# Mixer: the conformer branch goes last of the four, and its convolution taps are written one a step

## The chip, the cores and the metric

The kernel runs on one core of one Trainium2 chip. The metric is the device time of one execution in microseconds (us). The core has five engines that each take their own queue in order: TensorE (PE in the rows; PEld are its weight loads), VectorE (DVE), ScalarE (ACT), GpSimd (POOL) and SyncE (SP), which issues the loads of weights.

## The reference

A model of four layers on 256 tokens of width 1024. The first two layers are blocks of a feed-forward part, a mixer, and a feed-forward part; the last two are attention layers. The change lies in the mixer, which stands once in each of the first two layers:

```python
u = rms_norm(h, mix_pre_g[l])
(a_b, a_c, a_x, b_u, c_q, c_k, c_v,
 d_q, d_k, d_v, d_f, gate_logits) = _split(u @ w_in[l], IN_SPLITS)
y_a = short_conv_mixer(...)          # 3 taps
y_b = conformer_conv_mixer(...)      # 31 taps, then layer_norm, silu, output product
y_c = diff_attention_mixer(...)
y_d = forgetting_attention_mixer(...)
g = sigmoid(gate_logits)             # 4 x 1024 columns
merged = g[:, :, 0] * y_a + g[:, :, 1] * y_b + g[:, :, 2] * y_c + g[:, :, 3] * y_d
h = h + rms_norm(merged @ w_o[l], mix_post_g[l])
```

Branch b, the conformer branch:

```python
y = a * sigmoid(g)
y = causal_depthwise_conv(y, conv_w) + conv_b     # 31 taps over 512 channels
y = silu(layer_norm(y, ln_g, ln_b))
return y @ w_out
```

## The kernel before

**Products.** All large products run in a split form. `Stream` loads the weights in pieces of 128 x 1024 numbers in the order in which they are planned (four raw buffers, loads issued by SyncE), ScalarE rounds each piece to its high part `whi` (L95), VectorE subtracts to get the low part `wlo` (L96), and there are eight such pairs of buffers. A block of 128 tokens by 512 columns then takes three matmuls for each chunk of 128 rows: high by high, low by high, high by low (L396, L397, L399). A panel is 512 columns for both halves of the tokens (t = 0 and 1), that is two blocks; a block has eight chunks, or four for a branch's output product. The results stand in two PSUM banks of the pool `mm`; four other banks (`acc`) hold logits and attention outputs, two (`tr`) transposes.

**Steps.** Inside a block, `slot()` is called after every two chunks and at the end: that is one step. A step splits weights ahead, runs deferred work, and then has a purse: `RATE` = 0.8 is added, up to 1.6, and small pieces of work are taken from the list `work` (attention of c and d, the normalisation of b), and then from `filler`, as long as the purse is above 0. Each piece names its price in its `yield`. The convolution of b is the only filler: `conv_b` issues, for each of four channel blocks, one multiply (L615) and 30 taps (L617) on VectorE, with a `yield` behind each tap. When all are written, it starts `norm_b` for both halves of the tokens: transposes of the convolved tile `cb` (L624), statistics (L626, L628), a power on GpSimd (L263), normalised tile `lnx` (L631), transposes of it (L278), scale and shift (L637), tanh (L639, ScalarE), product (L643), and the high and low parts of `bt` (L292 on ScalarE, L293 on VectorE), which the output product of b reads.

**Order.** The mixer first computes its input panels, then for each branch in `BRANCHES`: a gate panel, an output panel, a second gate panel, a second output panel. After a branch's first gate panel, `finish(b)` writes all that is left of its work at once. The first branch writes the merged tile, the next two multiply by their gate on VectorE (L861) and add on GpSimd (L862), the last adds on VectorE and defers the transposes for the final product. The program as written gives each instruction its rank; the compiler that builds the engines' queues takes them by rank, but draws a later one forward where it finds the engine free and the instruction ready. What stands in a queue then runs in that order.

Of the kernel before, what the change touches and what calls it, by code (L numbers as in the profile page):

```python
# [29 lines left out]
RATE = 0.8  # L30
WINDOW = 8

BRANCHES = ["a", "d", "b", "c"]
GATE_OFF = {"a": 5640, "b": 5640 + DM, "c": 5640 + 2 * DM, "d": 5640 + 3 * DM}
FF_PANELS = [(i * 512, 512) for i in range(DFF // 512)]
FF_LAST = (DFF // 512 * 512, DFF % 512)
# [89 lines left out]
def encoder_kernel(ctx, tc, I, C, out, upto=None):  # L126
# [46 lines left out]
    def cols(w, c0, n):  # L173
        return (w[:, c0 : c0 + n], n)
# [9 lines left out]
    for l in range(DEPTH):  # L184
        plan_ffn(l, 1)
        for nm, (c0, n) in MIX_PANELS.items():
            W.plan((l, "m", nm), [cols(I["w_in"][l], c0, n)], KD)
        for b in BRANCHES:
            for i in range(2):
# [17 lines left out]
    def defer(fn, d=4):  # L207
        later.append((clock[0] + d, fn))
# [10 lines left out]
    def start(name, gens):  # L219
        work.extend([0, name, g] for g in gens)  # L220
# [15 lines left out]
    def finish(name):  # L236
        for q in (filler, work):
            while True:
                mine = [w for w in q if w[1] == name][:WINDOW]
                if not mine:  # L240
                    break
                for w in mine:
                    step(q, w)
# [58 lines left out]
    def to_T(src, X, t, c0=0, n=4, scale=None):  # L302

        p = tr_ps()
        tr(p, src, n)
        split_ps(c3(p, n), X[0][:, c0 : c0 + n, tb(t)], X[1][:, c0 : c0 + n, tb(t)], scale)
        X[2].update((c, t) for c in range(c0, c0 + n))
# [186 lines left out]
    def mixer(l, U, rs, tab, nxt):  # L494
# [116 lines left out]
        def conv_b():  # L611
            assert filled.count(30) == NTB
            cb = x4_p.tile([P, 4, SEQ], F32, tag="x4", name="cb")
            for c in range(4):
                V.tensor_scalar(out=cb[:, c], in0=yb[:, c, 0:SEQ], scalar1=cw[:, c, 0:1], scalar2=cw[:, c, 31:32], op0=ALU.mult, op1=ALU.add)  # L615
                for j in range(1, 31):
                    V.scalar_tensor_tensor(out=cb[:, c], in0=yb[:, c, j : j + SEQ], scalar=cw[:, c, j : j + 1], in1=cb[:, c], op0=ALU.mult, op1=ALU.add)  # L617
                    yield 0.33, 0
            start("b", [norm_b(cb, t) for t in range(NTB)])

        def norm_b(cb, t):
            p = tr_ps()
            for c in range(4):
                T.transpose(p[:, c * P : (c + 1) * P], cb[:, c, tb(t)], ident)  # L624
            bs = small("bst", 6)
            V.bn_stats(out=bs, in_=p)  # L626
            mv = small("bmv", 2)
            V.bn_aggr(out=mv, in_=bs)  # L628
            r = rpow(mv[:, 1:2], tag="ln")
            x = t2("lnx")  # L630
            V.tensor_scalar(out=x, in0=p, scalar1=mv[:, 0:1], scalar2=r, op0=ALU.subtract, op1=ALU.mult)  # L631
            yield 1.4, 4
            q = tr_ps()
            tr(q, x)
            v = t2("lnv")
            for c in range(4):
                V.tensor_scalar(out=v[:, tb(c)], in0=q[:, tb(c)], scalar1=cw[:, c, 32:33], scalar2=cw[:, c, 33:34], op0=ALU.mult, op1=ALU.add)  # L637
            th = t2("lnt")
            S.activation(th, v, AF.Tanh, scale=0.5)  # L639
            if "b" not in OT:  # L640
                OT["b"] = pair4("bt")
            yield 0.8, 1
            V.scalar_tensor_tensor(out=v, in0=th, scalar=1.0, in1=v, op0=ALU.add, op1=ALU.mult)  # L643
            split_ps(c3(v, 4), OT["b"][0][:, :, tb(t)], OT["b"][1][:, :, tb(t)], 0.5)
            OT["b"][2].update((c, t) for c in range(4))
            yield 1.2, 1
# [58 lines left out]

        panel(key("dv"), U, 520, ev_dv)
        filler.append([0, "b", conv_b()])
        panel(key("dq"), U, 512, ev_T(dqk[:, 0], "dq"))
        panel(key("dk"), U, 512, ev_T(dqk[:, 1], "dk"))
# [136 lines left out]
        MT = None  # L846
        for b in BRANCHES:
            for i in range(2):
# [7 lines left out]
                def ev_out(t, p):  # L856
                    m = M[:, t, sl]
                    if b == BRANCHES[0]:
                        V.scalar_tensor_tensor(out=m, in0=gt[t], scalar=1.0, in1=p, op0=ALU.add, op1=ALU.mult)
                    else:  # L860
                        V.scalar_tensor_tensor(out=gt[t], in0=gt[t], scalar=1.0, in1=p, op0=ALU.add, op1=ALU.mult)  # L861
                        (V if b == BRANCHES[-1] else G).tensor_tensor(out=m, in0=m, in1=gt[t], op=ALU.add)  # L862
                    if b == BRANCHES[-1]:
                        defer(lambda m=m, i=i: to_T(m, MT, t, c0=4 * i, scale=0.5), 3)

                panel(key("g" + b, i), U, 512, ev_gate)
                if i == 0:
                    finish(b)
                if b == BRANCHES[0] and i == 0:
                    M = b8_p.tile([P, NTB, DM], F32, tag="b8", name="merged")  # L870
# [440 lines left out]
```

## Time and profile before

| | |
|---|---|
| time, 3 runs | 1676.97 us median (1676.76 to 1680.42) |
| the profiled execution | 1680.77 us, of it span 1679.0 us |
| busy: TensorE, VectorE, ScalarE, GpSimd | 97%, 66%, 52%, 6% of the span |
| mean granted TensorE clock | 0.995 of full speed |

A busy share is an average over the span. What a wait costs is read on the engine that has no slack, TensorE here; the rows below show its waits in the mixer and the work of other engines beside them.

### The profile page before, as it was taken

How to read it: one execution, taken by the hardware profiler on the slowest of the kernel's cores; microseconds unless marked ns; L12 is line 12 of the kernel's file. 1: busy time of each engine (PE TensorE's matmuls, PEld its weight loads, DVE VectorE, ACT ScalarE, POOL GpSimd, SP SyncE). 2: the span in 40 equal slices, each digit the busy share in tenths (PEclk: the TensorE clock that was granted, in tenths of full speed). 3: DMA queues.
4: the chain of work that ended last, by engine and by line, in shares of the span. 5: the costliest groups of instructions: out<-in, count | busy, mean ns of one | idle time of the engine just before them, and what ended most of it. 6: DMA issues, size and time to landing. Idle time of an engine off the chain costs nothing. (4 is left out here: it accounts for less than half of the span.)

```text
span 1679.0 us, 21707 instructions
## 1 busy us (share of the span) xinstructions
PE 1631.7 (97%) x7949; PEld 1344.5 (80%) x7949; DVE 1114.2 (66%) x1802; ACT 871.9 (52%) x1349; POOL 108.9 (6%) x114
## 2 busy tenths in 40 slices
PE   7999999899999999999999998999999998999998
PEld 6888888778887888888887877788888887788686
DVE  6555566997666555565546599975665556887885
ACT  6544456564545454454535466644455445644653
POOL 0000000101100000000000010011010002100100
PEclk9999999999999999999999999999999999999999
DMA  7756556445665655566565573556475554533520
GB/s 272 228 183 204 170 178 202 130 119 183 190 200 173 213 180 197 152 225 198 174 205 182 150 226 101 168 193 191 153 233 174 188 196 133 177 97 114 151 76 26
DMA packets 141602, 289.83 MB, mean 173 GB/s; under 512 B 12374, under 2 KB 26478, under 8 KB 141240
## 3 DMA queue, kind: packets, MB, share of 16 engines
q1 hardware_dynamic: 140856, 285.82, 53.6%
q0 software_dynamic: 352, 2.11, 0.3%
q8 instruction: 62, 1.02, 0.2%
q10 hardware_dynamic: 288, 0.52, 0.1%
q14 instruction: 44, 0.36, 0.1%
HBM read 287.35 MB, written 1.06 MB: 172 GB/s over the span
## 5 line engine op out<-in xcount | busy, mean ns | idle before, releaser
L96 DVE TENSOR_TENSOR wlo<-raw,whi 128x1024 fp32r<-128x1024 f32 (+2 forms) x532 | 639.8, 1209 | 314.0 <-ACT whi L95 297.4
L95 ACT CAST whi<-raw 128x1024 fp32r<-128x1024 f32 (+2 forms) x532 | 547.8, 1036 | 407.5 <-PE mm L399 212.2
L396 PE MATMUL mm<-whi,uh 128*128 128x512 f32 (+2 forms) x1504 | 594.7, 396 | 1.8 <-ACT sq L1010 1.3
L399 PE MATMUL mm<-whi,ul 128*128 128x512 f32 (+2 forms) x1504 | 580.5, 386 | 0.4 <-DVE ul L293 0.4
L397 PE MATMUL mm<-wlo,uh 128*128 128x512 f32 (+2 forms) x1504 | 580.1, 386 | 0.0
L399 PEld LDWEIGHTS mm<-whi,ul 128*128 128x128 f32 x1504 | 283.5, 188 | 58.1 <-DVE ul L293 0.9
L396 PEld LDWEIGHTS mm<-whi,uh 128*128 128x128 f32 x1504 | 283.7, 189 | 57.8 <-issue 4.5
L397 PEld LDWEIGHTS mm<-wlo,uh 128*128 128x128 f32 x1504 | 284.1, 189 | 51.1 <-issue 1.0
L396 PE MATMUL acc<-whi,hth 128*128 128x512 f32 x352 | 137.4, 390 | 0.0
L397 PE MATMUL acc<-wlo,hth 128*128 128x512 f32 x352 | 137.0, 389 | 0.0
L617 DVE SCALAR_TENSOR_TENSOR cb<-yb,cw,cb 128x256 f32<-128x256 f32 x240 | 109.7, 505 | 0.5
L399 PE MATMUL acc<-whi,htl 128*128 128x512 f32 x352 | 108.8, 390 | 0.0
L397 PEld LDWEIGHTS acc<-wlo,hth 128*128 128x128 f32 x352 | 66.1, 188 | 13.7
L396 PEld LDWEIGHTS acc<-whi,hth 128*128 128x128 f32 x352 | 66.1, 188 | 13.7
L399 PEld LDWEIGHTS acc<-whi,htl 128*128 128x128 f32 x352 | 65.8, 188 | 13.5
L289 ACT CAST hth<-tr 128x512 fp32r<-128x512 f32 (+1 forms) x48 | 26.3, 548 | 63.4 <-PE tr L278 63.4
L475 DVE SCALAR_TENSOR_TENSOR hx<-mm,rs,sg 128x512 f32<-128x512 f32 x40 | 29.9, 746 | 43.3 <-PE mm L399 43.3
L263 POOL TENSOR_TENSOR post<-postm,nhalf 128x1 f32<-128x1 f32 x12 | 8.7, 724 | 743.9 <-DVE postm L259 743.9
L290 DVE TENSOR_TENSOR htl<-tr,hth 128x512 fp32r<-128x512 f32 (+1 forms) x48 | 30.8, 643 | 38.2 <-ACT hth L289 38.2
L854 ACT ACTIVATE gate<-mm,hrs 128x512 f32<-128x512 f32 x32 | 22.0, 687 | 47.5 <-PE mm L399 47.5
L270 ACT ACTIVATE junk<-acc 128x512 bf16<-128x512 f32 x24 | 14.1, 593 | 50.3 <-PE acc L399 50.3
L471 ACT ACTIVATE sg<-mm,rs 128x512 f32<-128x512 f32 x40 | 27.6, 690 | 17.7 <-PE mm L399 17.5
(356 smaller groups left out, 1674.7 us busy)
## 6 DMA issues: line engine op xcount, KB each, us to landing
raw<-in_w_in_dram SPq DMA_DIRECT2D x180, 512.0 KB
raw<-in_ffn_w_down_dram SPq DMA_DIRECT2D x88, 512.0 KB
raw<-in_ffn_w_gate_dram SPq DMA_DIRECT2D x80, 512.0 KB
raw<-in_ffn_w_up_dram SPq DMA_DIRECT2D x80, 512.0 KB
raw<-in_w_o_dram SPq DMA_DIRECT2D x16, 512.0 KB
raw<-in_w_out_dram SPq DMA_DIRECT2D x16, 512.0 KB
raw<-in_w_in_dram SPq DMA_DIRECT2D x16, 260.0 KB
raw<-in_ffn_w_gate_dram SPq DMA_DIRECT2D x16, 256.0 KB
```

Source lines behind the costliest of these rows:

```text
L95: self.nc.scalar.copy(hi[:, : ks * n], src)
L96: self.nc.vector.tensor_tensor(out=lo[:, : ks * n], in0=src, in1=hi[:, : ks * n].bitcast(F32), op=ALU.subtract)
L270: S.activation(j[:, :w], src, AF.Square, scale=scale, accum_out=acc)
L289: S.copy(hi, p)
L290: V.tensor_tensor(out=lo, in0=p, in1=hi.bitcast(F32), op=ALU.subtract)
L396: T.matmul(o, lhsT=X[0][:, xk, tb(t)], rhs=a, start=first, stop=False)
L397: T.matmul(o, lhsT=X[0][:, xk, tb(t)], rhs=b, start=False, stop=False)
L399: T.matmul(o, lhsT=X[1][:, xk, tb(t)], rhs=a, start=False, stop=last)
L471: S.activation(sg[t], p, AF.Silu, scale=rs[t])
L475: V.scalar_tensor_tensor(out=x, in0=p, scalar=rs[t], in1=sg[t], op0=ALU.mult, op1=ALU.mult)
L617: V.scalar_tensor_tensor(out=cb[:, c], in0=yb[:, c, j : j + SEQ], scalar=cw[:, c, j : j + 1], in1=cb[:, c], op0=ALU.mult, op1=ALU.add)
L854: S.activation(gt[t], p, AF.Tanh, scale=hrs[t])
```

## The change

Two lines. In `BRANCHES` the branches b and c change places, so that gate and output panels of b come last; the weights are planned by the same list. In `conv_b` the price of a tap goes from 0.33 to 0.75, so that with 0.8 a step about one tap is written in a step instead of two or three.

```diff
-BRANCHES = ["a", "d", "b", "c"]
+BRANCHES = ["a", "d", "c", "b"]
...
                 for j in range(1, 31):
                     V.scalar_tensor_tensor(out=cb[:, c], in0=yb[:, c, j : j + SEQ], scalar=cw[:, c, j : j + 1], in1=cb[:, c], op0=ALU.mult, op1=ALU.add)
-                    yield 0.33, 0
+                    yield 0.75, 0
```

On VectorE, at the first softmax of branch d (first mixer), where taps stand among weight splits (`wlo`) and the softmax instructions (L721, two rows for each of four heads), there stands before:

```order
L617 SCALAR_TENSOR_TENSOR cb<-yb,cw,cb 128x256 x3
L96 TENSOR_TENSOR wlo<-raw,whi 128x1024
L617 SCALAR_TENSOR_TENSOR cb<-yb,cw,cb 128x256 x13
L721 ISA de,dnm<-L,T_2153 128x256
L721 ISA dnm 128x1
L721 ISA de,dnm<-L,T_2153 128x256
L721 ISA dnm 128x1
L721 ISA de,dnm<-L,T_2153 128x256
L721 ISA dnm 128x1
L721 ISA de,dnm<-L,T_2153 128x256
L721 ISA dnm 128x1
L617 SCALAR_TENSOR_TENSOR cb<-yb,cw,cb 128x256
```

and now, from the same softmax to the next one:

```order
L617 SCALAR_TENSOR_TENSOR cb<-yb,cw,cb 128x256 x11
L721 ISA de,dnm<-L,T_2153 128x256
L721 ISA dnm 128x1
L721 ISA de,dnm<-L,T_2153 128x256
L721 ISA dnm 128x1
L721 ISA de,dnm<-L,T_2153 128x256
L721 ISA dnm 128x1
L721 ISA de,dnm<-L,T_2153 128x256
L721 ISA dnm 128x1
L617 SCALAR_TENSOR_TENSOR cb<-yb,cw,cb 128x256 x4
L615 TENSOR_SCALAR cb<-yb,cw 128x256
L617 SCALAR_TENSOR_TENSOR cb<-yb,cw,cb 128x256
```

Two taps fewer stand in the run ahead of the first softmax (39 in all since the first tap, 41 before), three more behind it (before: one tap, the multiply, one tap), and a weight split follows there that stood behind the second softmax before.

On TensorE, at the same place, transposes of the exponentials (`de`) and logits (`L`) stand among the matmuls of a panel (`mm`); before:

```order
L278 MATMUL tr<-ident,qk 128x128 x4
L748 MATMUL tr<-ident,de 128x128 x4
L717 MATMUL L<-dqk 128x128 x4
L396 MATMUL mm<-whi,uh 128x512
L397 MATMUL mm<-wlo,uh 128x512
L399 MATMUL mm<-whi,ul 128x512
L396 MATMUL mm<-whi,uh 128x512
L397 MATMUL mm<-wlo,uh 128x512
L399 MATMUL mm<-whi,ul 128x512
L748 MATMUL tr<-ident,de 128x128 x8
L717 MATMUL L<-dqk 128x128 x4
```

and now:

```order
L278 MATMUL tr<-ident,qk 128x128 x4
L396 MATMUL mm<-whi,uh 128x512
L397 MATMUL mm<-wlo,uh 128x512
L399 MATMUL mm<-whi,ul 128x512
L396 MATMUL mm<-whi,uh 128x512
L397 MATMUL mm<-wlo,uh 128x512
L399 MATMUL mm<-whi,ul 128x512
L748 MATMUL tr<-ident,de 128x128 x4
L717 MATMUL L<-dqk 128x128 x8
```

Six matmuls moved ahead of the first transposes of `de`, and the last four logits moved ahead of the next transposes of `de`. Between the first and the second set of logits twelve matmuls stand now, six before; behind the second set the numbers are the other way round, six ahead of the transposes of `qk` and twelve before.

On TensorE, at the normalisation of branch b, before (the matmuls are those of branch d's first output panel):

```order
L396 MATMUL mm<-whi,dt 128x512
L397 MATMUL mm<-wlo,dt 128x512
L399 MATMUL mm<-whi,dt 128x512
L624 MATMUL tr<-ident,cb 128x128 x8
L396 MATMUL mm<-whi,dt 128x512
L397 MATMUL mm<-wlo,dt 128x512
L399 MATMUL mm<-whi,dt 128x512
```

and now (the matmuls ahead are the last of b's first gate panel, those behind the first of b's output panel):

```order
L396 MATMUL mm<-whi,uh 128x512
L397 MATMUL mm<-wlo,uh 128x512
L399 MATMUL mm<-whi,ul 128x512
L624 MATMUL tr<-ident,cb 128x128 x8
L278 MATMUL tr<-ident,lnx 128x128 x8
L396 MATMUL mm<-whi,bt 128x512
L397 MATMUL mm<-wlo,bt 128x512
L399 MATMUL mm<-whi,bt 128x512
```

Before, 24 matmuls stand between the two sets of transposes and 114 between the second set and the first matmul that reads `bt`; now there is none in either place.

On VectorE, in the same normalisation, before:

```order
L96 TENSOR_TENSOR wlo<-raw,whi 128x1024 x5
L626 BN_STATS bst<-tr 128x6 x2
L628 BN_AGGR bmv<-bst 128x2
L861 SCALAR_TENSOR_TENSOR gate<-gate,mm 128x512
L261 TENSOR_SCALAR lnm<-bmv 128x1
L628 BN_AGGR bmv<-bst 128x2
L261 TENSOR_SCALAR lnm<-bmv 128x1
L631 TENSOR_SCALAR lnx<-tr,bmv,ln 128x512 x2
L861 SCALAR_TENSOR_TENSOR gate<-gate,mm 128x512
L96 TENSOR_TENSOR wlo<-raw,whi 128x1024 x2
L637 TENSOR_SCALAR lnv<-tr,cw 128x128 x8
```

and now:

```order
L96 TENSOR_TENSOR wlo<-raw,whi 128x1024 x4
L626 BN_STATS bst<-tr 128x6 x2
L628 BN_AGGR bmv<-bst 128x2
L96 TENSOR_TENSOR wlo<-raw,whi 128x1024
L261 TENSOR_SCALAR lnm<-bmv 128x1
L628 BN_AGGR bmv<-bst 128x2
L261 TENSOR_SCALAR lnm<-bmv 128x1
L631 TENSOR_SCALAR lnx<-tr,bmv,ln 128x512 x2
L637 TENSOR_SCALAR lnv<-tr,cw 128x128 x8
L643 SCALAR_TENSOR_TENSOR lnv<-lnt,lnv 128x512 x2
L293 SCALAR_TENSOR_TENSOR bt<-lnv,bt 128x4x128 x2
```

The two gating products (`gate`) are gone from the chain, one weight split stands in it instead, and the steps follow each other directly.

## Rows read from the trace of the kernel before

**Rows 1.** Page, part 1: busy us, share of span, instructions.
```profile
PE 1631.7 (97%) x7949; PEld 1344.5 (80%) x7949; DVE 1114.2 (66%) x1802; ACT 871.9 (52%) x1349; POOL 108.9 (6%) x114
```

**Rows 2.** Windows, first mixer: stretch, length, busy us by engine, PEclk, DMA.
```profile
223.00:448.00 225.00, 218.16 (x1109) 178.94 (x1108) 180.54 (x358) 130.26 (x227) 20.83 (x16) 0.98 0.53 165
```

**Rows 3.** Timeline, TensorE, d softmax: start, us, instruction, count, [idle before, releaser].
```profile
303.33 1.13 PE L717 MATMUL L<-dqk 64*128 64x256 f32 x8
...
305.99 1.14 PE L717 MATMUL L<-dqk 64*128 64x256 f32 x8
...
309.92 0.60 PE L278 MATMUL tr<-ident,qk 128*128 128x128 f32 x4
...
311.99 0.93 PE L748 MATMUL tr<-ident,de 128*128 128x128 f32 x4 [1.48 <-ACT de L722]
...
318.35 1.97 PE L748 MATMUL tr<-ident,de 128*128 128x128 f32 x8 [3.19 <-ACT cqk L313]
...
1009.63 0.93 PE L748 MATMUL tr<-ident,de 128*128 128x128 f32 x4 [1.53 <-ACT de L722]
...
1015.98 1.14 PE L748 MATMUL tr<-ident,de 128*128 128x128 f32 x8 [1.69 <-ACT cqk L313]
...
1021.08 0.66 PE L748 MATMUL tr<-ident,de 128*128 128x128 f32 x4 [1.75 <-ACT det L750]
```

**Rows 4.** Windows of low clock; the number before DMA share is PEclk.
```profile
318.00:324.80 6.80, 6.45 (x27) 5.21 (x27) 6.79 (x23) 5.82 (x16) 0.07 (x1) 0.50 0.68 192
...
1010.95:1014.30 3.35, 3.34 (x12) 2.01 (x8) 3.35 (x11) 2.91 (x10) 1.35 (x2) 0.51 0.02 5
```

**Rows 5.** Timeline, VectorE, d softmax, first layer.
```profile
305.74 5.22 DVE L617 SCALAR_TENSOR_TENSOR cb<-yb,cw,cb 128x256 f32<-128x256 f32 x13
...
310.89 0.41 DVE L721 CUSTOM_DVE_ANT_0 de<-L,T 128x256 f32<-128x256 f32 x1
...
312.66 1.37 DVE L615 TENSOR_SCALAR cb<-yb,cw 128x256 f32<-128x256 f32 x1
...
314.35 0.41 DVE L721 CUSTOM_DVE_ANT_0 de<-L,T 128x256 f32<-128x256 f32 x1
...
315.73 1.21 DVE L96 TENSOR_TENSOR wlo<-raw,whi 128x1024 fp32r<-128x1024 f32 x1
```

**Rows 6.** Timeline, GpSimd, same stretch.
```profile
312.42 1.47 POOL L741 TENSOR_TENSOR T<-T,tab 128x512 f32<-128x512 f32 x1 [11.88 <-DVE dnm L721]
```

**Rows 7.** Timeline, all engines, normalisation of branch b, first layer.
```profile
409.42 1.04 PE L624 MATMUL tr<-ident,cb 128*128 128x128 f32 x8
...
411.06 1.29 DVE L626 BATCH_NORM_STATS2 bst<-tr 128x6 f32<-128x512 f32 x2
...
412.35 0.65 DVE L861 SCALAR_TENSOR_TENSOR gate<-gate,mm 128x512 f32<-128x512 f32 x1
...
412.92 0.15 DVE L261 TENSOR_SCALAR lnm<-bmv 128x1 f32<-128x1 f32 x1
...
414.39 1.09 POOL L263 TENSOR_TENSOR ln<-lnm,nhalf 128x1 f32<-128x1 f32 x2
...
415.00 1.53 DVE L631 TENSOR_SCALAR lnx<-tr,bmv,ln 128x512 f32<-128x512 f32 x2 [1.66 <-POOL ln L263]
...
415.95 1.35 PE L278 MATMUL tr<-ident,lnx 128*128 128x128 f32 x8
...
417.06 0.47 PE L396 MATMUL mm<-whi,uh 128*128 128x512 f32 x1
...
420.42 2.63 DVE L637 TENSOR_SCALAR lnv<-tr,cw 128x128 f32<-128x128 f32 x8
...
422.97 1.47 DVE L643 SCALAR_TENSOR_TENSOR lnv<-lnt,lnv 128x512 f32<-128x512 f32 x2
...
424.19 1.14 ACT L292 ACTIVATE bt<-lnv 128x512 fp32r<-128x512 f32 x2
```

**Rows 8.** Timeline, TensorE, first matmul that reads b's result.
```profile
443.02 0.39 PE L396 MATMUL mm<-whi,bt 128*128 128x512 f32 x1
```

## The prediction

> **What bounds the kernel now.** I read the page's busy shares first: TensorE is busy 97% of the span and VectorE 66% [rows 1], so a change pays or costs only through time in which TensorE waits. Then the busy time by stretch: the mixer of the first layer, which is what the change touches, lies at about 223 to 448 us; TensorE is busy 218.16 of these 225.00 us [rows 2], so it stands idle 6.84 us, and all a better order could win back in a layer is that, and what the clock lost by it. Then the rows of TensorE with the waits ahead of them: in the first layer two waits in the softmax of branch d, 1.48 and 3.19 us, in the second layer three, 1.53, 1.69 and 1.75 us [rows 3]. Behind the waits the granted clock falls to the lower of its two levels: 0.50 for 6.80 us with 6.45 us busy in the first layer, 0.51 for 3.35 us with 3.34 us busy in the second [rows 4]. At half speed half of the busy time is lost: 3.2 and 1.7 us. The waits named and their clock are 4.67 + 4.97 + 4.9 = 14.5 us for both layers. That is the pot for a gain.
>
> The cause of these waits is VectorE: 13 taps in 5.22 us (0.40 us each) stand ahead of the first softmax instruction, which starts at 310.89 although its logits were issued at 303.33 [rows 3, 5].
>
> **The change part by part.** No instruction is added or removed; branch b's and c's weights, gate panels and output panels change places in the stream, with equal sizes, so SyncE issues the same loads of the same size in the same steps. There are two parts.
>
> *The thin spread.* A higher price per tap (0.75 for 0.33) writes the taps later in the program. But the order in which VectorE gets them hardly moves: the compiler draws ready taps forward into places where it thinks VectorE free. Ahead of the first softmax of d stand 39 taps instead of 41; the runs of 13 become runs of 14 and 11. So the softmax starts 2 x 0.40 = 0.8 us sooner, at 310.1, and its four instructions end at 311.5 (1.38 us, as from 314.35 to 315.73) [rows 5]. Behind it stand now five taps and the first multiply of a channel block (one tap, the multiply and one tap before), then a split, and then the second softmax. Six instructions at 0.40 us are 2.4 us; one of them is stretched, as the multiply is now, to 1.37 us while GpSimd's 1.47 us mask addition runs [rows 5, 6], 1.0 us more; the split is 1.21 us and the second softmax 1.38 us: its end comes at 311.5 + 3.4 + 1.2 + 1.4 = 317.5 instead of 315.7. On TensorE six more matmuls now stand ahead of the first transposes of the exponentials, so that wait (1.48 us) goes. But all eight last logits stand together behind them, and the second four need the banks that the second softmax empties. TensorE is there after two sets of logits and 24 matmuls: one set and six matmuls take 2.66 us (303.33 to 305.99), one set and twelve 3.93 us (to 309.92), so six more 1.27 us, in all 2 x 2.66 + 2 x 1.27 = 7.9 us [rows 3]; with two sets of transposes (0.60 and 0.93, the latter less the 0.2 in which the next row has begun) and four logits (0.3) that is 303.33 + 9.5 = 312.8 us. It waits 317.5 - 312.8 = 4.7 us there, against 4.67 us in two waits now. The wait changes its place and the transposes behind it may wait again, as the 1.75 us one does in the second layer; there the same working gives 4.7 us against 3.2 in the first two. Bounds: all 14.5 us gained, or 5 us more in each layer, if the new wait comes on top of the old ones rather than in their place. I take a loss of 1.0 us for both layers together, because VectorE, which is full there, has the same work before and after.
>
> *Branch b last.* Its normalisation hangs on the last tap, and the taps are over long before, around the first gate panel in both kernels. What moves is the chain from the convolved tile to the first output matmul of b. Now it runs beside matmuls of other branches: its transposes start at 409.42, and the first matmul that reads its result starts at 443.02, 17.7 us after the high part of the result is there at 425.33 [rows 7, 8]. It costs nothing. After the change it stands at the end of b's first gate panel, and on TensorE's queue nothing at all lies between: eight transposes of the convolved tile, eight of the normalised one, then the matmuls that read the result. TensorE takes its queue in order, so it waits for the whole chain. The last panel of matmuls holds both banks of the matmul pool until b's output blocks have them, so no later panel stands ahead either.
>
> The chain, from the start of the transposes, with the durations of [rows 7]: 1.64 us to the statistics (409.42 to 411.06, a weight split stands before them now too, and will). From the statistics to the first small instruction of the variance 1.86 us; in it lies a gating of 0.57 us (412.35 to 412.92), whose place a weight split of 1.21 us [rows 5] takes: 2.50 us. The power on GpSimd: 0.15 for the small instruction, 0.61 from its start to the normalising instruction (414.39 to 415.00), and 0.06 for the handover, 0.82 us. GpSimd's additions of merged tiles, in front of the power now, are gone from there: the last branch adds on VectorE. That is 4.96 us so far. 0.95 us to the transposes, half of their 1.35 us for one half of the tokens, 0.1 us handover: 6.7 us. 2.55 us from the scale and shift to the gating product (420.42 to 422.97): 9.25 us. Half of its 1.47 us, 0.08, half of the 1.14 us for the high part on ScalarE, and 0.14 to TensorE, as from the normalised tile to its transposes: 10.8 us. TensorE's own work in that time, which it has now too, is 1.04 + 1.11 us (415.95 to 417.06). So it is idle 10.8 - 2.15 = 8.65 us in a layer, 17.3 us in both. Little elsewhere can give it back: of the 6.84 us of idle time in the first mixer the two softmax waits are 4.67, so all other waits there together are 2.2 us.
>
> Bounds: without the splits in front of and inside the chain, and without the second half's scale and shift in front of the first half's product, 0.6 + 1.2 + 1.3 us less, 5.5 us a layer, 11 in all. Upwards, the transposes at half clock (1.1 more) and a split that waits for its load (some 1.5 us): 11.2 us a layer, 22.4 in all. I take 17.3, since each link has a row.
>
> *The clock.* The waits of the chain, about 4.9 and 3.5 us, are longer than those after which the clock falls now, so I expect it to fall here too. The price lies between nothing (the low stretch falls into the wait) and 3.2 us a layer, the longer stretch of [rows 4]. I take the shorter, 1.7 us: 3.3 us for both.
>
> The Trainium skill ("TensorE: Matmul & The Clock Gate", section "HAM oscillation — how this bites in real kernels") charges half of all throttled time when an engine starts cold after a wait. With the longer stretch of 6.80 us that would be 3.4 us a layer as an estimate by that page, 6.8 instead of 3.3 in the sum. The trace agrees as far as its two stretches show the lower level while TensorE is busy almost throughout; no run before the change shows a wait of 4 us in this place.
>
> **Sum.** 17.3 + 3.3 + 1.0 = 21.6 us. The profiled execution took 1680.77 us with a span of 1679.0; the runs shown have a median of 1676.97, 3.8 less. 1680.77 + 21.6 = 1702.4 for such an execution, and 1676.97 + 21.6 = 1698.6 us against the median: 1.3% slower.
>
> **Rivals.**
> 1. *The softmax waits go altogether.* For it: the first of them does lose its cause in the new order, and VectorE reaches the first softmax sooner. Against it: the eight logits now stand in front of a softmax that is later than before. Price: the pot of 14.5 us, against a chain of 17.3 us whose low clock falls into its waits: 1676.97 + 17.3 - 14.5 = 1679.8 us, no change. It decides for "not slower" from 13.9 us won back (17.3 less 0.2% of the time, 3.4 us).
> 2. *The softmax stretch gets worse.* The wait for the banks comes on top of waits of the transposes behind it, 5 us more in each layer: 1698.6 + 10 - 1 = 1707.6 us. For it: the transposes wait on copies that ScalarE does behind exponentials, as the 1.69 and 1.75 us waits do now. Against it: VectorE's work up to there is the same.
> 3. *The clock stays low longer after the chain,* as in the longer of the two stretches: 3.2 instead of 1.7 us a layer, 1701.6 us. For it: two waits within some 10 us. Against it: half of that time TensorE has nothing to lose.
>
> That the spread does not do what it says is part of the forecast, since the taps keep their places nearly.
>
> **How the numbers follow.** Forecast 0.68, rival 1 0.07, rival 2 0.13, rival 3 0.12. The range for 8 in 10 is 1688 to 1709: below, the chain at its lower bound with its clock (1676.97 + 11 less what the softmax may give), above, rival 2 with a little of rival 3. A measurement here tells about 0.2%, 3.4 us, from no change. Of rival 1 most is "no change": 0.05, and 0.02 for faster; the rest, 0.93, is slower.
>
> **What would show it.** In the profile after, each mixer should have two new waits of TensorE in a row: the transposes of the normalised tile for VectorE (about 4 to 5 us), and the first matmul that reads branch b's result for ScalarE's high part (3 to 4 us), with VectorE and GpSimd going through the chain in the durations above, and a stretch at 0.50 beside it. The 1.48 us wait ahead of the first transposes of the exponentials should be gone and one of about 5 us should stand at the last logits of d. The forecast is wrong if matmuls of a later panel run between the two sets of transposes, if the first matmul of b's result starts within 7 us of the first transposes, or if the softmax stretch of d loses its waits without new ones.

## The result, and the profile after

The changed kernel takes 1699.32 us (median of four runs, 1695.70 to 1700.53) against 1677.53 us of the kernel before on the same chip: a ratio of 1.0122, with a 95% interval of 1.0109 to 1.0135. The profiled execution took 1700.18 us with a span of 1698.4, which is 19.4 us over the span before.

The page's busy line, to be held against [rows 1]: the work on each engine is the same, and TensorE's busy time has grown by 6.3 us although it runs the same 7949 matmuls: the mean granted clock is 0.989 for 0.995.

```profile
PE 1638.0 (96%) x7949; PEld 1349.7 (79%) x7949; DVE 1110.9 (65%) x1802; ACT 872.2 (51%) x1349; POOL 112.4 (7%) x114
```

The waits of TensorE after, by what it waited for (total us, times, longest). The first and the last line lie in the softmax of d, the second and third in the normalisation of b; what is left out between lies outside the change.

```profile
PE L L717 <- DVE dnm L721: 8.6, 2, 4.3
PE tr L278 <- DVE lnx L631: 8.4, 2, 4.2
PE mm L396 <- ACT bt L292: 6.3, 2, 3.1
...
PE tr L748 <- ACT det L750: 2.9, 2, 2.1
```

The chain of b's normalisation in the first layer, all engines, from the timeline (start, us, engine, line, instruction, idle before and releaser); it answers to [rows 7, 8]:

```profile
472.61 1.03 PE L624 MATMUL tr<-ident,cb 128*128 128x128 f32 x8
...
473.68 1.29 DVE L626 BATCH_NORM_STATS2 bst<-tr 128x6 f32<-128x512 f32 x2
...
474.96 1.19 DVE L96 TENSOR_TENSOR wlo<-raw,whi 128x1024 fp32r<-128x1024 f32 x1
...
476.30 1.08 POOL L263 TENSOR_TENSOR ln<-lnm,nhalf 128x1 f32<-128x1 f32 x2 [10.54 <-DVE lnm L261]
...
476.89 1.53 DVE L631 TENSOR_SCALAR lnx<-tr,bmv,ln 128x512 f32<-128x512 f32 x2 [0.40 <-POOL ln L263]
477.85 1.94 PE L278 MATMUL tr<-ident,lnx 128*128 128x128 f32 x8 [4.21 <-DVE lnx L631]
478.98 2.64 DVE L637 TENSOR_SCALAR lnv<-tr,cw 128x128 f32<-128x128 f32 x8 [0.55 <-PE tr L278]
...
481.53 0.69 DVE L643 SCALAR_TENSOR_TENSOR lnv<-lnt,lnv 128x512 f32<-128x512 f32 x1
...
482.25 0.63 ACT L292 ACTIVATE bt<-lnv 128x512 fp32r<-128x512 f32 x1
...
482.93 0.79 PE L396 MATMUL mm<-whi,bt 128*128 128x512 f32 x1 [3.14 <-ACT bt L292]
...
1185.25 1.94 PE L278 MATMUL tr<-ident,lnx 128*128 128x128 f32 x8 [4.20 <-DVE lnx L631]
1190.33 0.79 PE L396 MATMUL mm<-whi,bt 128*128 128x512 f32 x1 [3.14 <-ACT bt L292]
```

Read it down: eight transposes, nothing on TensorE for 4.21 us, eight transposes, nothing for 3.14 us, then the matmul that took until 443.02 to come in the kernel before, with 114 matmuls of other panels ahead. VectorE goes from step to step without a pause longer than 0.55 us. The last two rows are the same two places in the second layer.

The clock falls behind these waits. Windows (stretch, length, busy time by engine, granted clock, DMA share, GB/s): the first is the chain's, the other two are in the softmax of d, as [rows 4].

```profile
477.70:487.90 10.20, 6.91 (x20) 5.42 (x21) 5.95 (x14) 2.43 (x4) 0.00 (x0) 0.51 0.12 41
317.00:320.40 3.40, 3.40 (x13) 2.79 (x13) 3.40 (x8) 3.40 (x10) 2.21 (x1) 0.51 0.75 210
1025.00:1031.80 6.80, 6.77 (x26) 5.25 (x24) 6.80 (x21) 6.11 (x19) 1.75 (x1) 0.61 0.60 183
```

The softmax of d, TensorE, after, as [rows 3]. The wait of 1.48 us ahead of the first transposes of the exponentials is gone, one of 4.32 us stands at the last logits in its place, and a wait for ScalarE's copy follows.

```profile
302.59 1.14 PE L717 MATMUL L<-dqk 64*128 64x256 f32 x8
...
316.77 1.56 PE L717 MATMUL L<-dqk 64*128 64x128 f32 x8 [4.32 <-DVE dnm L721]
...
325.19 0.66 PE L748 MATMUL tr<-ident,de 128*128 128x128 f32 x4 [2.06 <-ACT det L750]
...
407.33 0.39 PE L396 MATMUL mm<-whi,dt 128*128 128x512 f32 x1
...
1010.03 1.13 PE L717 MATMUL L<-dqk 64*128 64x256 f32 x8
...
1114.73 0.39 PE L396 MATMUL mm<-whi,dt 128*128 128x512 f32 x1
```

The first matmul that reads `dt` lies behind the same work in both kernels, so the time from the first logits to it prices the softmax stretch. The rows of before for it:

```profile
408.06 0.39 PE L396 MATMUL mm<-whi,dt 128*128 128x512 f32 x1
...
1000.93 1.13 PE L717 MATMUL L<-dqk 64*128 64x256 f32 x8
...
1104.72 0.39 PE L396 MATMUL mm<-whi,dt 128*128 128x512 f32 x1
```

First layer: 408.06 - 303.33 [rows 3] = 104.73 us before, 407.33 - 302.59 = 104.74 after. Second layer: 103.79 before, 104.70 after. The softmax stretch costs 0.0 + 0.9 us. From the first logits of layer 1 to those of layer 2 are 697.60 us before and 707.44 after, 9.84 us more, all of it behind the softmax. From there to the end of the span are 678.07 us before (1679.0 - 1000.93) and 688.37 after, 10.30 us more, 0.9 of it the softmax. So the chain with its clock costs some 9.8 and 9.4 us; the 0.7 us that the first layer started earlier goes off, and 19.4 us are left.

What the clock has of that is read from TensorE's busy time (the first number behind the length) behind the softmax, from the first matmul that reads `dt` to the next logits, in the second layer to the end of the span. Before:

```profile
408.06:1000.93 592.87, 589.41 (x2738) 486.57 (x2736) 358.94 (x427) 295.91 (x361) 31.02 (x26) 1.00 0.59 190
1104.72:1679.00 574.28, 553.15 (x2809) 458.31 (x2807) 387.60 (x690) 289.95 (x502) 52.55 (x62) 0.99 0.47 149
```

and after:

```profile
407.33:1010.03 602.70, 592.56 (x2737) 488.96 (x2736) 356.05 (x427) 296.47 (x361) 33.55 (x26) 0.99 0.58 186
1114.73:1698.40 583.67, 556.17 (x2809) 460.39 (x2807) 386.42 (x690) 290.49 (x502) 53.27 (x62) 0.99 0.47 147
```

The same matmuls (one record in 2738 apart) keep TensorE busy 3.15 and 3.02 us longer, 6.2 us in both layers. I read that as the clock's price, since the trace shows nothing else that slows them. Its idle time there grew by 6.68 and 6.37 us, a little less than the 7.35 and 7.34 us of the chain's two waits, since other waits became 0.7 and 1.0 us shorter.

### The profile page after: what moved, and what is told of

Its sections match the earlier page's. It is cut to its first block, busy times and chain, and to the rows that moved or that the text cites. A ratio compares the mean times of both kernels' runs of the same rounds, so it can differ in the third digit from the quotient of the medians.

```text
span 1698.4 us, 21691 instructions
## 1 busy us (share of the span) xinstructions
PE 1638.0 (96%) x7949; PEld 1349.7 (79%) x7949; DVE 1110.9 (65%) x1802; ACT 872.2 (51%) x1349; POOL 112.4 (7%) x114
```

## The experiments

Ratios are to the kernel before on the same chip, with 95% intervals. The changed kernel was measured once more beside the first three:

> The changed kernel once more, as a control on the chip of this call: 1697 to 1701 us by either theory.

It gave 1699.27 us against 1677.74, ratio 1.0130 (1.0116 to 1.0144).

**1. The order alone.** Branch b last, the tap at its old price.

```diff
 BRANCHES = ["a", "d", "c", "b"]
...
-                    yield 0.75, 0
+                    yield 0.33, 0
```

> Branch b last, with the old price of 0.33 a tap. Theory (the loss is the chain of b's normalisation, which stands bare on TensorE's queue at the end of b's first gate panel): it stays, and only what the spread does to the softmax of d goes, so 1697 to 1700 us, within 2 us of the changed kernel, with the two waits of about 4.2 and 3.1 us in each mixer. Rival (the thin spread costs the time, since VectorE runs taps late): 1677 to 1680 us.

Measured: 1677.71 us against 1677.74, ratio 0.9999 (0.9990 to 1.0008). My theory is wrong. The timeline shows why: with b last, the normalisation is still written beside d's output panel, and there is no wait ahead of its transposes.

```profile
407.95 1.04 PE L624 MATMUL tr<-ident,cb 128*128 128x128 f32 x8
...
414.49 1.34 PE L278 MATMUL tr<-ident,lnx 128*128 128x128 f32 x8
```

**2. The price alone.** Branch b third as before, the tap at 0.75.

```diff
 BRANCHES = ["a", "d", "b", "c"]
...
-                    yield 0.33, 0
+                    yield 0.75, 0
```

> The old order a, d, b, c with the new price of 0.75 a tap. Theory: the compiler draws taps forward anyway, and the softmax waits only change their place: 1676 to 1680 us (about +1, as the softmax stretch of the changed kernel measures). Rival (the spread costs): 1690 us or more. Second rival (the spread frees VectorE for the softmax): 1665 to 1672 us.

Measured: 1700.91 us, ratio 1.0137 (1.0120 to 1.0154): the whole loss, and the rival's case. The same two waits stand in it, behind b's gate panel, wherever that panel is:

```profile
444.64 1.94 PE L278 MATMUL tr<-ident,lnx 128*128 128x128 f32 x8 [4.20 <-DVE lnx L631]
...
449.73 0.80 PE L396 MATMUL mm<-whi,bt 128*128 128x512 f32 x1 [3.14 <-ACT bt L292]
```

**3. The changed kernel with the chain written one panel earlier.** The rest of b's work is written ahead of its first gate panel, so that the panel's 48 matmuls rank behind the chain and can be run beside it.

```diff
+                if b == BRANCHES[-1] and i == 0:
+                    finish(b)
                 panel(key("g" + b, i), U, 512, ev_gate)
```

> The changed kernel, but what is left of branch b is written ahead of its first gate panel instead of behind it, so that matmuls of that panel can run beside the normalisation. Theory: the two waits and their low clock go (about 9.8 us a layer), the small loss in the softmax stretch stays: 1677 to 1681 us. Rival (b last costs by itself, for instance by VectorE adding merged tiles or by the output panels' order): 1688 us or more.

Measured: 1679.74 us, ratio 1.0009 (1.0000 to 1.0018), as expected. The chain's waits are nearly gone, and the softmax wait of 4.3 us a layer stays, so what the softmax stretch costs is in these 2 us and nearly all of the rest was the chain:

```profile
PE L L717 <- DVE dnm L721: 8.6, 2, 4.3
...
PE tr L278 <- DVE lnx L631: 0.7, 2, 0.4
```

With these three a new theory was at hand. A step puts 0.8 into the purse; attention takes its pieces first, then the taps are written for what they cost, and only when the last tap is written is `norm_b` started. Following the program's steps from the start of the taps: at the end of d's first gate panel 72 steps are over, of the third branch's 96, of the last one's 120. The attention pieces have cost 18.04 by then. With the old price all taps (39.6) are written within the 72 steps and both normalisations in the next 24, in pieces among matmuls. At 0.75 and b third, 60.0 of 90 are spent at step 96, so 80 of 120 taps are written; with b last 79.5 at step 120, 106 taps. `finish(b)` then writes the other taps and the whole normalisation in one lump, behind b's gate panel. The compiler draws those taps forward, so that they are long done by then, but not the transposes: they stand behind the gate panel's matmuls on TensorE's queue, with nothing between them and b's output. By this theory the position of b decides only between the prices at which 96 steps don't do for the taps and 120 do (the normalisation, written in steps, takes some more): (120 x 0.8 - 18.04)/120 = 0.65 and (96 x 0.8 - 18.04)/120 = 0.49. The next two runs are at 0.55, between the two.

**4. A price of 0.55, b last, and the same with b third.**

```diff
-                    yield 0.75, 0
+                    yield 0.55, 0
```

> Branch b last, as in the changed kernel, but a tap costs 0.55. Theory of the purse: a step gives 0.8, and at the end of b's first gate panel (some 120 steps after the taps were started) 96 have been given; the taps ask 120 x 0.55 = 66 and the attention pieces some 18, 84 in all, so the normalisation is written in steps among matmuls ahead of that panel's end and no wait of 4.2 or 3.1 us stands in it: 1676 to 1681 us. Rival, a dearer tap costs by itself, whatever becomes of the normalisation (two thirds of the way from 0.33 to 0.75, a half of the loss or more): 1687 to 1698.

> The same tap price of 0.55 with branch b third, as in the kernel before. Theory of the purse: only some 96 steps lie ahead of the end of b's first gate panel, 77 have been given, the taps and attention ask 84, so the normalisation is written in one lump behind that panel, its transposes wait 4.2 us and the first matmul of b's output 3.1 us in each layer: 1696 to 1702 us. Rival, the price alone decides: the same time as the run with b last at 0.55.

Measured, on one chip: b last 1683.88 us, ratio 1.0036 (1.0024 to 1.0048); b third 1699.76 us, ratio 1.0130 (1.0117 to 1.0143). 15.9 us lie between two kernels with the same price, and the sign of the position is the opposite of what I had forecast: at this price b last is the better place, because it leaves the purse 24 more steps. The chain with b last, where the transposes of the normalised tile come in two fours among matmuls, and with b third:

```profile
460.22 0.60 PE L278 MATMUL tr<-ident,lnx 128*128 128x128 f32 x4
...
462.56 0.63 PE L278 MATMUL tr<-ident,lnx 128*128 128x128 f32 x4 [1.50 <-DVE lnx L631]
...
476.41 0.39 PE L396 MATMUL mm<-whi,bt 128*128 128x512 f32 x1
```

```profile
445.57 1.94 PE L278 MATMUL tr<-ident,lnx 128*128 128x128 f32 x8 [4.20 <-DVE lnx L631]
...
450.65 0.79 PE L396 MATMUL mm<-whi,bt 128*128 128x512 f32 x1 [3.14 <-ACT bt L292]
```

The run with b last is 3 us over what I expected and 5.9 us over the kernel before. I had not foreseen the waits of 1.50 and 1.46 us in its two chains. The softmax of d takes longer too: from the first logits to the first matmul that reads `dt` are 104.98 and 105.52 us, 2.0 us more than before in both. The waits can't simply be added, though: from the first logits of layer 1 to those of layer 2 its profiled execution is only 0.42 us longer than that of the kernel before, and 5.25 us from there to the end, so most of the loss lies in and behind the second mixer. Where the rest of it went is open.

**5. TensorE kept busy in the chain's waits.** The changed kernel with 26 more matmuls a mixer, 16 ahead of the transposes of the normalised tile and 10 behind them, whose results nobody reads. On TensorE's queue 17 came to stand ahead of these transposes, one between their two fours and eight behind.

```diff
+        def idle(n):
+            d = acc_ps("idle")
+            for _ in range(n):
+                T.matmul(d, lhsT=U[0][:, 0, 0:P], rhs=U[0][:, 0:2, :].rearrange("p k s -> p (k s)"), start=True, stop=True)
...
+            if t == NTB - 1:
+                idle(16)
             yield 1.4, 4
             q = tr_ps()
             tr(q, x)
+            if t == NTB - 1:
+                idle(10)
```

> The changed kernel with 26 matmuls more in each mixer, whose result nobody reads, put into the two waits of the normalisation (17 behind the first set of transposes, 9 around and behind the second). The chain keeps its length, TensorE's clock has no reason to fall. Theory (the low clock behind the waits costs 2.5 to 3 us a layer beside the waits): 1693 to 1696 us, and no stretch at 0.50 beside the chain. Rival (the low stretch falls into the waits and costs nothing): 1698 to 1701 us.

Measured: 1697.19 us against 1678.39, ratio 1.0107 (1.0094 to 1.0121): some 3 us less than the changed kernel's 1.0130, with intervals that overlap a little, so the gain is not clear of noise. It lies between the two expectations. The windows of the same 22 us around the chain, with the unread matmuls and in the changed kernel, show that the clock came back in part, 0.92 for 0.77:

```profile
472.00:494.00 22.00, 20.20 (x90) 15.62 (x90) 16.49 (x30) 7.28 (x10) 1.08 (x2) 0.92 0.38 120
```

```profile
472.00:494.00 22.00, 14.65 (x61) 11.67 (x60) 15.80 (x29) 7.14 (x10) 1.08 (x2) 0.77 0.34 112
```

The unread matmuls did not fill the second wait, though, and the matmuls behind it still run at the lower clock:

```profile
482.61 0.50 PE L396 MATMUL mm<-whi,bt 128*128 128x512 f32 x1 [1.44 <-ACT bt L292]
```

```profile
484.00:486.00 2.00, 2.00 (x6) 1.54 (x6) 0.13 (x1) 0.00 (x0) 0.00 (x0) 0.50 0.00 0
```

So this run does not take the low stretch away; it moves it behind the second wait and makes it shorter. Its gain of some 3 us is a part of the clock's price, not the whole, which by the busy time above is some 6.2 us. The larger part of the loss is the waiting in the chain, which stays nearly as long with the clock up: 9.87 us from the first transposes to the first matmul that reads `bt` (472.74 to 482.61), for 10.32.

**6. Three taps instead of thirty,** in the kernel before. It leaves out 27 of the 30 taps in each channel block, so its output is not the reference's; it asks what VectorE's load is worth.

```diff
-                for j in range(1, 31):
+                for j in range(1, 4):
```

> The kernel before with 3 taps instead of 30 in each channel block: 108 taps a layer left out, so the convolution isn't the reference's. Theory (the softmax waits of d and their low clock come from taps that stand ahead on VectorE): 1663 to 1668 us, the waits of 1.48, 3.19, 1.53, 1.69 and 1.75 us gone. Rival (the waits are the softmax's own chain from logits to exponentials): 1674 to 1677 us.

Measured: 1687.82 us, ratio 1.0057 (1.0044 to 1.0069): 94 us of VectorE's work less, and slower. Both expectations miss. The waits in d's softmax shrink to 1.3 us each, but the normalisation, written when the last tap is, now comes in the input panels, and its transposes wait there. The waits by what TensorE waited for, and the one in the first layer:

```profile
PE tr L278 <- DVE lnx L631: 11.4, 2, 6.2
PE tr L624 <- DVE cb L617: 6.7, 2, 3.4
```

```profile
301.06 1.11 PE L278 MATMUL tr<-ident,lnx 128*128 128x128 f32 x4 [5.25 <-DVE lnx L631]
```

It is the same lesson from the other end: the price and the number of taps set where the chain is written, and the 18.1 us that TensorE waits there outweigh what the softmax gains.

**7. Better versions?** Three tries to free d's softmax of the taps, all with b last: b's input panels and the taps behind those of c and d, with the chain written ahead of b's gate panel, at 0.75; the same at 0.45; and b's input panels between c's query and key panels, at 0.45.

```diff
-        panel(key("bg"), U, 512, ev_bg)
-        panel(key("ba"), U, 512, ev_ba)
...
-        filler.append([0, "b", conv_b()])
...
         panel(key("cv"), U, 512, ev_cv)
+        panel(key("bg"), U, 512, ev_bg)
+        panel(key("ba"), U, 512, ev_ba)
+        for _ in range(5):
+            slot()
+        filler.append([0, "b", conv_b()])
...
+                if b == BRANCHES[-1] and i == 0:
+                    finish(b)
```

> Order a, d, c, b with 0.75 a tap; b's two input panels moved behind those of c and d, so that no tap can run before the softmaxes, and b's remainder written ahead of its first gate panel. Theory: VectorE is free for the softmaxes of d and c, the taps run beside the gate and output panels of a, d and c, and the normalisation beside b's gate panel: 1663 to 1669 us, faster than both kernels. Rival (the taps then hold up splits of weights beside the gate panels): 1677 us or more.

> The run with b's input panels behind those of c and d again, b last, but a tap costs 0.45. Theory: with the dear tap two waits per layer ate the gain, 3.7 us of the transposes of the convolved tile for the last tap and 2.0 us of b's output for a gate; a cheaper tap ends the taps and the normalisation earlier among matmuls, so both go, 11 us in all, with the smaller softmax waits of that order kept: 1667 to 1672 us. Rival, the taps then stand ahead of the softmaxes again and bring the old waits back: 1676 to 1682.

> The last run with b's two input panels moved up, between c's query and key panels, and the taps started ahead of c's value panel, some 20 us earlier; b last, a tap costs 0.45. Theory: in the last run the 7.3 us of waits of output blocks for a gating product come from VectorE being full of taps (110 of 120 us between 330 and 450 us); taps that start earlier leave it some room there, and they still stand behind most of d's softmax, so these waits shrink without new ones: 1668 to 1674 us. Rival, the room on VectorE only changes its place and c's softmax now waits behind taps: 1675 to 1680 us.

Measured: 1680.24 us, ratio 1.0011 (1.0002 to 1.0021); 1675.61 us, 0.9988 (0.9979 to 0.9998); 1676.02 us, 0.9992 (0.9982 to 1.0001). None comes to what I expected: the times of the first and the third are those of their rivals, and the second lies between, just below its rival's. The waits of TensorE in the three (lines are up to three off here: L623 is the transposes of the convolved tile, L746 d's transposes of the exponentials, L864 or L862 the gating product; the L746 line is the same in all three):

```profile
PE tr L623 <- DVE cb L616: 7.4, 2, 3.7
...
PE mm L397 <- DVE gate L864: 4.1, 4, 1.8
PE tr L746 <- ACT cqk L314: 3.4, 2, 1.7
```

```profile
PE mm L397 <- DVE gate L864: 7.3, 4, 2.6
```

```profile
PE mm L397 <- DVE gate L862: 7.0, 4, 1.9
```

d's softmax waits fall to 1.7 us a layer in all three. Instead the gate panels behind the output panels of d and c wait for a gating product, which stands behind taps and weight splits on VectorE. The second is 0.1% faster than the kernel before, hardly more than can be measured; in none are TensorE's waits on VectorE gone, they only move.

## Why the prediction was right, and where it was wrong

The time and the mechanism were forecast; the part of the change that brings it was not. The signs that were named are in the profile after: waits of 4.2 us (4 to 5 were named) and 3.1 us (3 to 4) in the chain, a stretch at 0.51 beside them, and 4.3 us (about 5) at the last logits of d.

- **The failed step is the paragraph "Branch b last".** It had the chain right and what moves it wrong. It said that the chain moves behind b's first gate panel because b comes last, and that "the taps are over long before". The taps are over on VectorE, but not in the program as written, and it is there that `norm_b` is started. Experiments 1, 2 and 4 show the price to be the cause: the old price with b last costs nothing, the new price with b third costs all of it, and at 0.55 b last loses 15.9 us less than b third.
- **"The thin spread" was read on the wrong engine.** "The order in which VectorE gets them hardly moves" is right for the taps, and the price of 1.0 us for the softmax stretch met 0.9 us. But the paragraph looked at the taps' order alone and did not follow what hangs on the last of them. The order of the changed kernel, which I had, contains both edits, so it could not tell which of them moved the chain; one of the two applied alone would have. That the total came right although the wrong edit was held to bring it is owed to that order: it showed the chain's new place, whatever had put it there.
- **The chain's length was nearly met.** 10.8 us were forecast from the transposes to the first matmul, 10.32 measured (472.61 to 482.93). TensorE's own work in it was put at 2.15 us and is 2.97, mostly since the transposes of the normalised tile run at the lower clock (1.94 us for 1.35, [rows 7]), so the waits are 7.35 us a layer, not 8.65: 14.7 in both, not 17.3. The split of 1.21 us inside the chain is where it was said to be (474.96). No split waited for its load there; the 1.5 us put down for one in the upper bound are shown by no run.
- **The clock's term was too small.** 1.7 us a layer were taken, the shorter stretch of [rows 4]. The busy time of the same matmuls grew by 3.15 and 3.02 us, 6.2 in both for 3.3, and that includes the slow transposes. The low stretch is 10.20 us long, longer than the two of [rows 4], but TensorE is busy 6.91 us of it only. The section "HAM oscillation — how this bites in real kernels" of the Trainium skill's "TensorE: Matmul & The Clock Gate" counts half of the throttled time; half of the 10.20 us would be 5.1 us a layer as an estimate by it, half of the 6.91 busy us 3.5. The 3.15 and 3.02 us of the trace lie near the second: part of the stretch lies in the second wait, where a low clock costs nothing. The prediction's estimate by that page, 6.8 us in the sum, was nearer than the 3.3 us that it took.
- **The sum came out closer than its terms, and that is luck.** 14.7 + 6.2 + 0.9 us, less the 1.6 us by which other waits shrank and the 0.7 us of the earlier start, make 19.5 us in the profiled execution (19.4 unrounded) against 21.6 forecast. The waits were 2.6 us too high and the clock 2.9 us too low, which cancels; the 1.6 and 0.7 us had no term. The medians differ by 21.8 us, 2.4 more than the profiled executions; that is chance in the runs, not working.
- **The rivals.** The first (softmax waits vanish) is excluded by the 4.3 us waits, the second (softmax worse by 5 us a layer) by the 0.0 and 0.9 us. The third (the clock low for longer) is what happened to the clock: 3.1 us a layer by the busy time, near its 3.2 and not the forecast's 1.7. That the time is nearer the forecast's all the same comes from the shorter waits of the chain.

## What to carry to other kernels

The price of a filler in such a scheduler decides not only how thinly the filler lies but when its end is written, and with it everything that starts only there: reckon the sum of prices against the steps that are left until the point where the rest is written at once, and look there at what stands between the links of the chain on the engine that has no slack. A compiler that draws ready instructions forward hides this, because the filler itself runs early and only its successor is late. If a change has two edits, follow each alone through the program before giving one of them the price.

## What was not expected of the hardware

From the end of a wait of 4.2 us TensorE ran at the lower clock for a stretch of 10.2 us, through a second wait of 3.1 us, and eight transposes of 128 x 128 took 1.94 us in it for 1.35 before. Unread matmuls, most of them in the first wait, brought the mean clock of the 22 us around the chain from 0.77 to 0.92; the clock then fell behind the second wait, of which 1.44 us were left (0.50 from 484 to 486 us).

VectorE's first multiply of a channel block took 1.37 us before [rows 5], beside a GpSimd addition of 1.47 us [rows 6]; after, the same multiply takes 0.40 us at 313.75, and the stretching, which the forecast had taken for 1.0 us, has moved to the taps that now lie beside the addition, as the rows of VectorE and GpSimd after show (four taps in 2.69 us, where eleven take 4.44):

```profile
305.40 4.44 DVE L617 SCALAR_TENSOR_TENSOR cb<-yb,cw,cb 128x256 f32<-128x256 f32 x11
...
311.13 2.69 DVE L617 SCALAR_TENSOR_TENSOR cb<-yb,cw,cb 128x256 f32<-128x256 f32 x4
313.75 0.40 DVE L615 TENSOR_SCALAR cb<-yb,cw 128x256 f32<-128x256 f32 x1
```

```profile
311.30 1.46 POOL L741 TENSOR_TENSOR T<-T,tab 128x512 f32<-128x512 f32 x1 [11.09 <-DVE dnm L721]
```
